# Hybrid encoder layer: a fixed order of operations and a fixed buffer for each tile in place of a list scheduler

## The chip, the cores and the metric

The kernel runs on one core of a Trainium2 chip. The metric is the time of one execution on the device in microseconds (us), the median over runs. The engines are TensorE (PE, with its weight loads as PEld), VectorE (DVE), ScalarE (ACT), GpSimd (POOL) and SyncE (SP), which issues most of the transfers. PSUM is the memory that PE writes, eight banks of 2 KB per partition; tiles lie in SBUF.

## The reference

One layer (SEQ 512, D_MODEL 1024, float32) of an encoder with two branches side by side, then a feed-forward part (FFN):

```python
h = rmsnorm(x, mix_norm)
p = h @ w_in
rx, ry, qkv, z, ba, gates = jnp.split(p, SPLIT_IDX, axis=-1)
y_rnn = rglru_branch(rx, ry, ...) @ w_rnn_proj     # conv, gates r and i, two linear scans (forward, backward)
y_dn = deltanet_branch(qkv, z, ba, ...) @ w_dn_proj
g_rnn, g_dn = jnp.split(jax.nn.sigmoid(gates), 2, axis=-1)
x = x + (g_rnn * y_rnn + g_dn * y_dn) @ w_out
h = rmsnorm(x, ffn_norm)
gt, up = jnp.split(h @ w_gate_up, 2, axis=-1)
x = x + (jax.nn.silu(gt) * up) @ w_down
return rmsnorm(x, final_norm)
...
# deltanet_branch, for each of 8 heads and 2 directions, over chunks of the sequence:
A = jnp.where(strict, jnp.einsum("nhcid,nhcjd->nhcij", kb, k) * decay, 0.0)
u = triangular_solve(A + eye, v * beta)            # unit lower triangle
w = triangular_solve(A + eye, kb * exp(gc))
S = S * exp(gl) + kd^T @ (u - w @ S)               # step from chunk to chunk
```

## The kernel before, in words

The whole layer is one function, `trunk`, with no loops left on the chip: about nine thousand operations in one long program. Each weight of 128 columns is loaded as 512 KB of float32 (`wraw`), ACT casts it to a rounded half (`hi`, in a `wx` or `t4` tile) and DVE makes the rest (`lo = raw - hi`). A product is then three matmuls, hi by hh, hi by hl and lo by hh, where `hh` and `hl` are the same two halves of the normalised and transposed input. The output projection and the two FFN products use forms with seven instead of eight partial products, whose sums of weight and input blocks are made on DVE; partial sums pass through DRAM tensors named `sums` and `osums`.

Where the program is in the chip's time:
- up to about 25 us, the head: four tiles of x are loaded, normalised, transposed on PE (`ax <- ident, t`) and split into hh and hl; `mm120` is the first input projection, `mm62` the narrow one of 32 columns for the DeltaNet's gates.
- to about 630 us, the input projections, and between them the recurrent branch and, head by head, the DeltaNet. Its triangular inverse (`dn_inverse`) stands at about 320, 420, 500 and 590 us: DVE solves 32-row blocks, then PE joins them in products of 32 by 32 and 64 by 64 (`ax <- t,na`, `ax <- t,t`), each step needing DVE or ACT to bring the result of the step before into SBUF. Other products with 512 columns stand between the steps as cover.
- to about 720 us, the output projections.
- from 720 to 940 us, gate and up (`in_w_gate_up`) with 256-column products, and with them the weights' sums; from 940 the down product, the last norm and the output.

No engine's order is that of the source. Each call on an engine goes through a recorder (`Rec`, line 384 for all of them, so that the profile groups by tiles and not by lines), which keeps the operation with a cost. `Plan.order` is a list scheduler: it plays the program through with those costs, with a lag from engine to engine, with the price of a table change on ACT, and with the transfers' time; whenever an engine is free, it picks among its ready operations the one with the earliest due time, if the tiles that it needs can be had. The due times come from a table by stage (`TIMES`), less 12 us (`AHEAD`) for the cast of a weight and 40 us for its load. The operations are then issued in that order, and the tile pools give each new tile a buffer of its kind and make it wait for the release of the buffer's last tile.

The kinds, with their numbers of buffers (`t2` holds 2 KB per partition, `t4`, `wraw` and `wx` 4 KB; `mm`, `ax` and `st` are banks of PSUM):

```python
N2, N4, NW = 15, 24, 4
...
raw = new(wp, shape, "wraw", NW)
hi = new(wp, shape, "wx", 4, F32R)
...
return new(ps, (P, 512), "mm", 3)
return new(ps, (P, 512), "ax", 3)
return new(ps, (P, 512), "st", 2)
```

A tile's name in the listings below is its kind, a running number and the number of the tensor (mm120_200); the same running number after the change is the same tile (ps120_197). In the profile the numbers are left out.

Of the kernel before, what the change touches and what calls it, by code (L numbers as in the profile page):

```python
# [7 lines left out]
F32 = mybir.dt.float32  # L8
# [22 lines left out]
SWITCH = 12000  # L31
WARM = 3400
RELEASE = 200
LOOK = 40
TIMES = [
# [14 lines left out]
]  # L50
ENGINES = ("PE", "DVE", "ACT", "POOL", "SP")
N2, N4, NW = 15, 24, 4
AHEAD = 12.0
# [6 lines left out]
class Plan:  # L60

    TABLES = {AF.Exp: ("exp",), AF.Tanh: ("exp", "sigmoid", "silu", "gelu"), AF.Sigmoid: ("sigmoid",), AF.Sqrt: ("sqrt",),
              AF.Ln: ("ln",), AF.Silu: ("silu",), AF.Gelu_apprx_tanh: ("gelu",)}

    LAG = {("PE", "PE"): 0, ("PE", "DVE"): 250, ("PE", "ACT"): 250, ("DVE", "PE"): 320, ("ACT", "PE"): 320, ("POOL", "PE"): 320,
           ("DVE", "DVE"): 130, ("DVE", "ACT"): 250, ("ACT", "ACT"): 50, ("ACT", "DVE"): 200, ("DVE", "POOL"): 250,
           ("POOL", "DVE"): 150, ("ACT", "POOL"): 250, ("SP", "SP"): 0}

    def __init__(self, nc):
        self.nc = nc
        self.ops = []
        self.where, self.bases = [], []
        self.t = self.base = 0.0
        self.stage = 0
        self.tags = {}
        self.tile_tag = {}
        self.hist = {}
        self.keep = set()  # L80
        self.extra = ()
        self.admit = ()

    def tile(self, pool, shape, dt, tag, bufs, name):
        ap = pool.tile(list(shape), dt, tag=tag, name=name, bufs=bufs)
        self.tile_tag[ap.tensor.name] = tag
        self.tags[tag] = bufs
        return ap

    @staticmethod  # L90
    def region(ap):
        t = ap.tensor
        name = t.name
        dims = list(ap.ap)
        if ap.space == PSUM:
            return name, 0, P, 1
        if ap.space == DRAM:
            lo = hi = ap.offset
            for s, n in dims:
                lo, hi = (lo, hi + s * (n - 1)) if s >= 0 else (lo + s * (n - 1), hi)  # L100
            return name, lo, hi + 1, 1
        pitch = 1
        for n in t.shape[1:]:
            pitch *= n
        p0, off = divmod(ap.offset, pitch)
        free = [(s, n) for s, n in dims[1:] if s != 0 and n > 1]
        free.sort(key=lambda d: abs(d[0]))
        starts, run = [off], 1
        for s, n in free:
            if s < 0:  # L110
                starts, s = [x + s * (n - 1) for x in starts], -s
            if s <= run:
                run = s * (n - 1) + run
            else:
                starts = [x + s * i for x in starts for i in range(n)]
        gran = max(1, pitch // 256)
        mask = 0
        for x in starts:
            a, b = x // gran, (x + run - 1) // gran
            mask |= ((1 << (b - a + 1)) - 1) << a  # L120
        return name, p0, p0 + dims[0][1], mask

    def add(self, eng, fn, outs, ins, cost, tail=0.0, table=None):
        i = len(self.ops)
        deps = set(self.extra)
        touched = {ap.tensor.name for ap in self.admit}
        for aps, write in ((ins, False), (outs, True)):
            for ap in aps:
                name, p0, p1, mask = self.region(ap)
                if name not in self.tile_tag and name not in self.keep:  # L130
                    continue
                touched.add(name)
                h = self.hist.setdefault(name, [])
                for j, q0, q1, m, w in h:
                    if (write or w) and j != i and q0 < p1 and p0 < q1 and m & mask:
                        deps.add(j)
        for aps, write in ((ins, False), (outs, True)):
            for ap in aps:
                name, p0, p1, mask = self.region(ap)
                if name not in self.tile_tag and name not in self.keep:  # L140
                    continue
                h = self.hist[name]
                if write:
                    h[:] = [r for r in h if not (p0 <= r[1] and r[2] <= p1 and r[3] | mask == mask) or r[0] == i]
                h.append((i, p0, p1, mask, write))
        self.ops.append((eng, fn, deps, touched, round(cost), round(1.25 * tail), table, self.t))
        self.where.append((self.stage, round(1e3 * (self.t - self.base))))
        self.bases.append(round(1e3 * self.base))

    def order(self):  # L150
        import heapq
        from bisect import insort
        ops = self.ops
        n = len(ops)
        when = []
        for (s, d), b in zip(self.where, self.bases):
            if s < len(TIMES):
                b, b0 = TIMES[s] * 100, b
            elif TIMES:
                b += max(TIMES) * 100 - b0  # L160
# [1578 lines left out]
```

## Time and profile before

| | us |
|---|---|
| median of 3 runs | 1052.1 (1052.09 to 1052.18) |
| span of the profiled execution, first to last instruction | 1051.0 |
| PE busy | 1037.1 (99%) |
| PEld busy | 905.0 (86%) |
| DVE busy | 869.5 (83%) |
| ACT busy | 706.7 (67%) |
| POOL busy | 75.7 (7%) |

Of the profiled execution the span is what the profile gives, and the durations below come from it. A matmul's end in the profile is modelled, so that its record is longer than the distance to the next one; the distance between starts is what a matmul costs in a dense stretch. Rows of groups give the operation, its output and inputs, its shape and number, the busy time and mean duration, and the idle time of the engine before it with its releaser. Rows of windows give the stretch and the busy time of PE, PEld, DVE, ACT and POOL (number of instructions in brackets), the granted clock, the share of the transfer engines and GB/s. Rows of the timeline and of the chain begin with the start and the duration.

### The profile page before, as it was taken

How to read it: one execution, taken by the hardware profiler on the slowest of the kernel's cores; microseconds unless marked ns; L12 is line 12 of the kernel's file. 1: busy time of each engine (PE TensorE's matmuls, PEld its weight loads, DVE VectorE, ACT ScalarE, POOL GpSimd, SP SyncE). 2: the span in 40 equal slices, each digit the busy share in tenths (PEclk: the TensorE clock that was granted, in tenths of full speed). 3: DMA queues.
4: the chain of work that ended last, by engine and by line, in shares of the span. 5: the costliest groups of instructions: out<-in, count | busy, mean ns of one | idle time of the engine just before them, and what ended most of it. 6: DMA issues, size and time to landing. Idle time of an engine off the chain costs nothing.

```text
span 1051.0 us, 17876 instructions
## 1 busy us (share of the span) xinstructions
PE 1037.1 (99%) x6707; PEld 905.0 (86%) x6707; DVE 869.5 (83%) x1626; ACT 706.7 (67%) x1287; POOL 75.7 (7%) x133
## 2 busy tenths in 40 slices
PE   8999999999999999999999999999999999999997
PEld 7888788888888987887888798889999999998886
DVE  7769989669794697489469657999999898989997
ACT  7799989787537877686875644668544454556574
POOL 2000000204100220211021000000000000000000
PEclk9999999999999999999999999999999999999999
DMA  9622222245233256559536564688453644336532
GB/s 278 196 79 81 61 75 75 71 112 148 81 100 91 73 144 150 158 133 218 122 76 145 169 172 140 197 256 292 129 171 102 200 139 130 109 110 207 197 123 80
DMA packets 180854, 146.95 MB, mean 140 GB/s; under 512 B 6784, under 2 KB 161552, under 8 KB 180768
## 3 DMA queue, kind: packets, MB, share of 16 engines
q1 hardware_dynamic: 175840, 129.95, 41.8%
q0 software_dynamic: 3744, 12.72, 6.5%
q10 hardware_dynamic: 1184, 3.15, 0.8%
q8 instruction: 52, 0.85, 0.3%
q14 instruction: 34, 0.28, 0.1%
HBM read 121.12 MB, written 12.09 MB: 127 GB/s over the span
## 4 chain that ended last, share of the span: by engine, by line
PE 86%; DVE 8%; ACT 2%; DMA 2%; issue 1%; SPq 1%; ACTq 0%; DVEq 0%
PE mm L384 49%; PE ax L384 23%; PE st L384 15%; DVE t L384 6%; ACT t L384 1%; DVE na L384 1%; DVE wx L384 1%; SPq L384 1%; DMA t<-in_w_down_dram 1%; DMA wraw<-in_w_in_dram 1%; DMA gain2r<-in_ffn_norm_dram 0%; ACT wx L384 0%; ACT ax L384 0%; ACTq L384 0%; ACT na L384 0%
## 5 line engine op out<-in xcount | busy, mean ns | idle before, releaser
L384 PE MATMUL mm<-hh,wx 128*128 128x512 f32 (+2 forms) x1280 | 368.8, 363 | 0.1
L384 DVE TENSOR_TENSOR t<-t,t 128x512 fp32r<-128x512 f32 (+25 forms) x501 | 249.3, 511 | 30.3 <-ACT t L384 20.7
L384 PEld LDWEIGHTS mm<-hh,wx 128*128 128x128 f32 (+1 forms) x1280 | 230.4, 188 | 35.4 <-ACT wx L384 0.7
L384 PE MATMUL mm<-hl,wx 128*128 128x512 f32 (+2 forms) x648 | 228.6, 362 | 0.0
L384 ACT CAST wx<-wraw 128x1024 fp32r<-128x1024 f32 (+3 forms) x139 | 129.9, 937 | 90.6 <-PE mm L384 32.9
L384 PE MATMUL ax<-t,t 128*128 128x512 f32 (+3 forms) x1134 | 156.9, 292 | 1.2 <-DVE t L384 1.2
L384 DVE TENSOR_TENSOR wx<-wraw,wx 128x1024 fp32r<-128x1024 f32 (+3 forms) x115 | 120.7, 1051 | 35.5 <-PE mm L384 16.8
L384 PEld LDWEIGHTS ax<-t,t 128*128 128x128 f32 (+1 forms) x1134 | 123.0, 161 | 21.6 <-issue 2.2
L384 PEld LDWEIGHTS mm<-hl,wx 128*128 128x128 f32 (+1 forms) x648 | 121.7, 188 | 16.8
L384 ACT CAST t<-t 128x512 fp32r<-128x512 f32 (+2 forms) x148 | 94.1, 653 | 44.5 <-DVE t L384 36.1
L384 PE MATMUL mm<-t,wx 128*128 128x512 f32 x480 | 116.6, 394 | 0.0
L384 PEld LDWEIGHTS mm<-t,wx 128*128 128x128 f32 x480 | 89.0, 188 | 18.4 <-issue 0.2
L384 DVE SCALAR_TENSOR_TENSOR t<-mm,par,t 128x511 f32<-128x511 f32 (+1 forms) x108 | 80.2, 744 | 20.9 <-ACT t L384 19.7
L384 ACT ACT_TABLE_LOAD x64 | 82.1, 1283 | 5.0 <-DVE t L384 2.3
L384 PE MATMUL mm<-t,t 128*128 128x256 f32 (+1 forms) x420 | 79.8, 330 | 0.1
L384 ACT ACTIVATE t<-t 128x128 f32<-128x128 f32 (+4 forms) x86 | 47.5, 559 | 41.0 <-DVE t L384 39.3
L384 PEld LDWEIGHTS mm<-t,t 128*128 128x128 f32 x420 | 63.8, 190 | 7.2 <-DVE t L384 0.5
L384 PE MATMUL st<-hh,wx 128*128 128x512 f32 (+1 forms) x224 | 67.7, 375 | 0.0
L384 ACT CAST t<-wraw 128x1024 fp32r<-128x1024 f32 (+1 forms) x55 | 49.2, 894 | 18.3 <-DMA wraw<-in_w_gate_up_dram 7.2
L384 DVE TENSOR_TENSOR t<-wraw,t 128x1024 fp32r<-128x1024 f32 (+1 forms) x55 | 56.3, 1023 | 5.3 <-ACT t L384 5.1
L384 PEld LDWEIGHTS st<-hh,wx 128*128 128x128 f32 x224 | 41.2, 188 | 7.6
L384 PE MATMUL st<-hl,wx 128*128 128x512 f32 (+1 forms) x112 | 41.5, 375 | 0.0
(195 smaller groups left out, 1519.1 us busy)
## 6 DMA issues: line engine op xcount, KB each, us to landing
wraw<-in_w_in_dram SPq DMA_DIRECT2D x72, 512.0 KB, 4.1
wraw<-in_w_gate_up_dram SPq DMA_DIRECT2D x44, 512.0 KB, 4.1
wx<-wraw POOLq DMA_DIRECT2D x24, 512.0 KB, 5.3
wraw<-in_w_out_dram SPq DMA_DIRECT2D x12, 512.0 KB, 4.5
wraw<-in_w_rnn_proj_dram SPq DMA_DIRECT2D x16, 384.0 KB, 3.5
t<-in_w_down_dram SPq DMA_DIRECT2D x11, 512.0 KB, 5.9
sums<-t SPq DMA_DIRECT2D x11, 512.0 KB, 5.0
wraw<-sums SPq DMA_DIRECT2D x11, 512.0 KB, 3.6
```

What stands on the lines that cost most here:

```text
L384: self.plan.add(e, lambda: real(*a, **kw), outs, ins, cost, tail, table)
```

## The change

The scheduler, its costs, its due times and all arguments that fed it (`after`, `admit`, `spend`, `ahead`) are taken out. In their place stand two tables. `ORDER` lists the numbers of the 9123 recorded operations in the order in which they are issued; by the change's own words it was searched with random transfer and vector delays. `HOMES` gives each tile of the kinds t2, t4 and PSUM one buffer by number: 16 homes of 2 KB, 32 of 4 KB, and 8 banks. The raw weights and their halves are now t4 tiles like the others (4 + 4 + 24 buffers before, 32 in one set after), and mm, ax and st are one set of eight banks (3 + 3 + 2 before). A home is a pool with one buffer; the program itself adds, for each engine that begins to use the buffer's new tile, a wait for the other engines' last use of the old one. The operations and their shapes are the same on every engine, apart from the waits and the table loads of ACT that the order entails: 74 of them instead of 64 in the listings. PE has 144 separate instructions for semaphore waits instead of 58.

```diff
-SWITCH = 12000
-WARM = 3400
-RELEASE = 200
-LOOK = 40
-TIMES = [
-    -162283, -159297, -163526, -108037, -92752, -158970, -94346, -59098, 168648, -70151, -72611, -51972, -22916,
...
-N2, N4, NW = 15, 24, 4
-AHEAD = 12.0
+ORDER = """
+2 15 16 17 18 19 0 126 5 3 7 122 20 21 22 23 24 10 12 11 8 283 1 25 26 27 28 13 14 29 30 9 129 31 32 33 34 111 127 113
...
+HOMES = """
...
-    def order(self):
...
+    def place(self, pool, shape, dt, home, name):
+        ap = pool.tile(shape, dt, tag=home, name=name, bufs=1)
+        self.home[ap.tensor.name] = home
+        return ap
+
+    def emit(self):
+        order = [int(i) for i in ORDER.split()]
...
+        info = mybir.DependencyInfo(mybir.DependencyClass.Sync, mybir.DependencyReason.ANTI)
+        now, users, before = {}, {}, {}
+        for i in order:
+            eng, names, run = self.ops[i]
+            ins = run().ins
+            for name in names:
+                home = self.home.get(name)
+                if home is None:
+                    continue
+                if now.get(home) != name:
+                    now[home] = name
+                    before[home], users[home] = users.get(home, {}), {}
+                if eng not in users[home]:
+                    for other, last in before[home].items():
+                        if other != eng:
+                            self.tc.add_manual_dep(ins, last.name, info, reason="the buffer's last use")
+                users[home][eng] = ins
...
     def new(pool, shape, tag, bufs, dt=F32):
-        return plan.tile(pool, shape, dt, tag, bufs, nm(tag))
+        if tag in ("t2", "t4", "ps"):
+            return plan.place(pool, list(shape), dt, f"{tag}h{next(homes)}", nm(tag))
+        return pool.tile(list(shape), dt, tag=tag, name=nm(tag), bufs=bufs)
...
-        return new(ps, (P, 512), "mm", 3)
+        return new(ps, (P, 512), "ps", 1)
...
     with tc.manual_schedule():
-        todo = plan.order()
-        for i in todo:
-            plan.ops[i][1]()
+        plan.emit()
```

Three places, as the listings of the two programs have them.

The first place is the head. On SP, before (t4117's raw weight is `wraw117`, that of the narrow projection `wraw60`; t411 to t414 are the tiles of x):

```order
1 L384 DMA t411_91<-in_x_dram 128x1024
2 L384 DMA t412_92<-in_x_dram 128x1024
3 L384 DMA wraw117_197<-in_w_in_dram 128x8x128
4 L384 DMA t413_93<-in_x_dram 128x1024
5 L384 DMA t414_94<-in_x_dram 128x1024
6 L384 DMA t2121_201<-in_rg_wa_dram 128x2x128
7 L384 DMA t2121_201<-in_rg_wx_dram 128x2x128
8 L384 DMA wraw60_140<-in_w_in_dram 128x8x32
9 L384 DMA wraw132_212<-in_w_in_dram 128x8x128
10 L384 DMA t2136_216<-in_rg_wa_dram 128x2x128
```

On SP, after:

```order
1 L508 DMA t411_88<-in_x_dram 128x1024
2 L508 DMA t412_89<-in_x_dram 128x1024
3 L508 DMA t4117_194<-in_w_in_dram 128x8x128
4 L508 DMA t460_137<-in_w_in_dram 128x8x32
5 L508 DMA t414_91<-in_x_dram 128x1024
6 L508 DMA t413_90<-in_x_dram 128x1024
7 L508 DMA t4132_209<-in_w_in_dram 128x8x128
8 L508 DMA t4102_179<-in_w_in_dram 128x8x128
9 L508 DMA t2136_213<-in_rg_wa_dram 128x2x128
```

The narrow weight moved from the eighth place to the fourth, ahead of the last two tiles of x, which changed places, and the recurrent gates' weights moved behind two more projections' weights. On PE in the head, before, from the last of the first twelve transposes on:

```order
14 L384 MATMUL ax35_115<-ident1_81,t428_108 128x128
15 L384 MATMUL mm120_200<-hh19_99,t4118_198 128x256
16 L384 MATMUL mm120_200<-hl20_100,t4118_198 128x256
17 L384 MATMUL mm120_200<-hh19_99,t4118_198 128x256
18 L384 MATMUL mm120_200<-hl20_100,t4118_198 128x256
19 L384 MATMUL ax36_116<-ident1_81,t421_101 128x128
20 L384 MATMUL ax36_116<-ident1_81,t428_108 128x128
```

On PE in the head, after, from the last transposes of the first two tiles on:

```order
17 L508 MATMUL ps35_112<-ident1_78,t421_98 128x128
18 L508 MATMUL ps35_112<-ident1_78,t428_105 128x128
19 L508 MATMUL ps120_197<-hh19_96,t4118_195 128x256
20 L508 MATMUL ps62_139<-hh19_96,t461_138 64x256
21 L508 MATMUL ps62_139<-hl20_97,t461_138 64x256
22 L508 MATMUL ps62_139<-hh19_96,t461_138 64x256
23 L508 MATMUL ps120_197<-hl20_97,t4118_195 128x256
24 L508 MATMUL ps120_197<-hh19_96,t4118_195 128x256
```

All sixteen transposes of the first two tiles now stand ahead of the first projection, and the narrow projection's products (ps62) stand between its products instead of behind them.

The second place is the first step of the triangular inverse in the first of its four places, on PE; before (bank 495 holds the first product of the step, bank 497 the second, which needs it in SBUF as t2496):

```order
1113 L384 MATMUL ax495_575<-t2492_572,na479_559 32x32
1114 L384 MATMUL ax495_575<-t2493_573,na479_559 32x32
1115 L384 MATMUL mm445_525<-t4414_494,wx447_527 128x512 x2
1116 L384 MATMUL mm445_525<-t4420_500,wx447_527 128x512 x2
1117 L384 MATMUL ax497_577<-t2493_573,t2496_576 32x32
1118 L384 MATMUL ax497_577<-t2492_572,t2496_576 32x32
```

And after:

```order
1181 L508 MATMUL ps495_572<-t2493_570,na479_556 32x32
1182 L508 MATMUL ps473_550<-t4408_485,t4476_553 128x512
1183 L508 MATMUL ps473_550<-t4414_491,t4476_553 128x512
1184 L508 MATMUL ps473_550<-t4420_497,t4476_553 128x512
1185 L508 MATMUL ps473_550<-t4432_509,t4476_553 128x512
1186 L508 MATMUL ps473_550<-t4438_515,t4476_553 128x512
1187 L508 MATMUL ps473_550<-t4444_521,t4476_553 128x512
1188 L508 MATMUL ps560_637<-hh19_96,t4559_636 128x512 x4
1189 L508 MATMUL ps498_575<-t2496_573,t2493_570 32x32
```

Four products of 512 columns stood between the two steps, and ten do now; the two banks that the second step fills (497 and 498) are now filled together.

The third place is in the FFN, on PE, where one bank (1684) gets two products one after the other and DVE empties it in between. Before, from the end of the first one to the begin of the second:

```order
3685 L384 MATMUL ax1684_1764<-t41217_1297,t41678_1758 128x256 x4
3686 L384 MATMUL ax1683_1763<-hh1082_1162,t41677_1757 128x256
...
3694 L384 MATMUL ax1683_1763<-hh1082_1162,t41678_1758 128x256 x4
3695 L384 MATMUL mm1659_1739<-hh1082_1162,wx1651_1731 128x256
3696 L384 MATMUL mm1659_1739<-hl1083_1163,wx1651_1731 128x256
3697 L384 MATMUL ax1684_1764<-t41223_1303,t21679_1759 128x256
```

After, the end of the first product in bank 1684, and the begin of the second:

```order
4024 L508 MATMUL ps1684_1761<-t41217_1294,t41678_1755 128x256 x2
4025 L508 MATMUL ps1683_1760<-t41219_1296,t41675_1752 128x256
...
4098 L508 MATMUL ps1660_1737<-t41221_1298,t41654_1731 128x256 x2
4099 L508 MATMUL ps1681_1758<-hh1082_1159,t41674_1751 128x256
4100 L508 MATMUL ps1684_1761<-t41223_1300,t21679_1756 128x256
```

Fourteen products of 256 columns stood between the two uses of the bank, and now some 76 rows do.

More of the change, by code (lines that the diff above doesn't have):

```diff
@@ L28 @@
 EPS = 1e-6
-SWITCH = 12000
-WARM = 3400
-RELEASE = 200
-LOOK = 40
-TIMES = [
[14 rows of a table removed]
-]
-ENGINES = ("PE", "DVE", "ACT", "POOL", "SP")
-N2, N4, NW = 15, 24, 4
-AHEAD = 12.0
+ORDER = """
[387 rows of a table added]
+"""
+HOMES = """
[37 rows of a table added]
+"""
 LASTK = 3
@@ L60 @@
 class Plan:
[L64 to L87, printed above, removed]
-        return ap
@@ L90, in region @@
[L90 to L130, printed above, removed]
-                    continue
[L132 to L148, printed above, removed]
@@ L318, in elems, with __init__ @@
-def elems(ap):
-    n = 1
-    for s, m in list(ap.ap)[1:]:
-        n *= m
-    return n
+    def __init__(self, tc):
+        self.tc, self.ops, self.home = tc, [], {}
+    def place(self, pool, shape, dt, home, name):
+        ap = pool.tile(shape, dt, tag=home, name=name, bufs=1)
+        self.home[ap.tensor.name] = home
+        return ap
+    def emit(self):
+        order = [int(i) for i in ORDER.split()]
+        if sorted(order) != list(range(len(self.ops))):
+            raise RuntimeError("the order is not one of these operations")
+        info = mybir.DependencyInfo(mybir.DependencyClass.Sync, mybir.DependencyReason.ANTI)
[6 more added lines that the diff above has]
+                if home is None:
+                    continue
+                if now.get(home) != name:
[6 more added lines that the diff above has]
+                users[home][eng] = ins
@@ L334, in call @@
         def call(*a, **kw):
-            args = list(a) + list(kw.values())
-            aps = [x for x in args if hasattr(x, "ap") and hasattr(x, "tensor")]
-            out = kw.get("out", a[0] if a else None)
-            outs = [out] + ([kw["accum_out"]] if kw.get("accum_out") is not None else [])
-            ins = [x for x in aps if not any(x is o for o in outs)]
-            big = [x for x in ins if elems(x) > 1 or x.space == PSUM]
-            n = max([elems(out)] + [elems(x) for x in ins])
@@ L384, in call @@
-            self.plan.add(e, lambda: real(*a, **kw), outs, ins, cost, tail, table)
+            names = {x.tensor.name for x in list(a) + list(kw.values()) if hasattr(x, "ap") and hasattr(x, "tensor")}
+            self.plan.ops.append((self.eng, names, lambda: real(*a, **kw)))
         return call
@@ L1202, in out_sums @@
     def out_sums(j):
-        spend(0.1)
-        now = plan.t
-        ra, rb, s_ = new(wp, (P, 2, 512), "wraw", NW), new(wp, (P, 2, 512), "wraw", NW), four()
-        plan.t = now - 40
+        ra, rb, s_ = new(t4, (P, 2, 512), "t4", 1), new(t4, (P, 2, 512), "t4", 1), four()
         Q.dma_start(ra, wo[:, j, 0, :].rearrange("p (h n) -> p h n", h=2))
         Q.dma_start(rb, wo[:, j, 1, :].rearrange("p (h n) -> p h n", h=2))
-        plan.t = now
         V.tensor_tensor(s_[:, 0, :], ra[:, 0, :], ra[:, 1, :], ALU.add)
@@ L1228, in trunk @@
             dn_z(g)
-        spend()
         dn_out(g)
@@ L1310, in halves @@
     def halves(src, own=False):
-        hi, lo = (new(wp, (P, 2, 512), "wx", 4, F32R) if own else four(F32R) for _ in range(2))
-        parts_of(src, hi, lo, 0)
+        hi, lo = (new(t4, (P, 2, 512), "t4", 1, F32R) if own else four(F32R) for _ in range(2))
+        parts_of(src, hi, lo)
         return [(hi[:, i, :], lo[:, i, :]) for i in range(2)]
     def out_w(j):
-        now = plan.t
-        ra, rs = new(wp, (P, 2, 512), "wraw", NW), new(wp, (P, 2, 512), "wraw", NW)
-        plan.t = now - 40
+        ra, rs = new(t4, (P, 2, 512), "t4", 1), new(t4, (P, 2, 512), "t4", 1)
         Q.dma_start(ra[:, 0, :], wo[:, j, 0, 0:512])
@@ L1465, in gate_up @@
     def gate_up(n):
-        spend(10.2)
-        now = plan.t
-        rg, ru = new(wp, (P, 8, P), "wraw", NW), new(wp, (P, 8, P), "wraw", NW)
-        plan.t = now - 40
+        rg, ru = new(t4, (P, 8, P), "t4", 1), new(t4, (P, 8, P), "t4", 1)
         Q.dma_start(rg, wg[:, :, n * P:(n + 1) * P])
```

440 lines of the change are left out of this document (69 added, 371 removed), and 436 rows, old and new, of tables (HOMES, ORDER, TIMES).

## The prediction

> **What bounds the kernel now.** I read the page first, then the windows of 25 us, the chain that ended last, the groups by shape, and last the timeline at the places where the windows show the PE short. The head of the page:
>
> ```profile
> span 1051.0 us, 17876 instructions
> PE 1037.1 (99%) x6707; PEld 905.0 (86%) x6707; DVE 869.5 (83%) x1626; ACT 706.7 (67%) x1287; POOL 75.7 (7%) x133
> PEclk9999999999999999999999999999999999999999
> PE 86%; DVE 8%; ACT 2%; DMA 2%; issue 1%; SPq 1%; ACTq 0%; DVEq 0%
> ```
>
> The span is 1051.0 us and the median of the runs 1052.1, so 1.1 us lie outside the span; I keep them. PE is busy nearly all the time at the full clock in every slice. The change leaves every PE instruction as it is, so the first question is how much of the 1051.0 an order can touch at all. For that the busy share is no use, because a matmul's end is modelled; I use the distance between matmuls in dense stretches, from the chain:
>
> ```profile
> 277.53 45.33 PE mm L384 x200
> 748.64 2.88 PE mm L384 x24
> ```
>
> The first is 200 products of 512 columns: 45.33/200 = 0.227 us each. The second is 24 products of 256 columns: 0.120 us each. The groups by shape give the counts (first and last of the nine 512-column groups, then the largest of 256 and the small ones):
>
> ```profile
> L384 PE MATMUL mm<-hh,wx 128*128 128x512 f32 x912 | 293.6, 395 | 0.1
> L384 PE MATMUL st<-wx,t 128*128 128x512 f32 x90 | 23.2, 389 | 0.0
> L384 PE MATMUL mm<-hh,wx 128*128 128x256 f32 x352 | 70.8, 283 | 0.0
> L384 PE MATMUL ax<-ident,t 128*128 128x128 f32 x178 | 27.3, 275 | 0.7 <-DVE t L384 0.5 <-ACT ax L384 0.2
> L384 PE MATMUL ax<-t,t 32*32 32x32 f32 x384 | 4.9, 196 | 0.0
> ```
>
> All groups of a kind together: 2901 products of 512 columns make 657.7 us, 2066 of 256 columns 247.9, 64 slow ones of 256 columns about 14, and 758 of 128 columns with the 896 small tiles about 97 (0.11 each by their starts, 0.01 to 0.03 for the small ones). The sum is 1016 us of work that no order removes. The first useful transpose and the last products of the program:
>
> ```profile
> 7.51 0.69 PE L384 MATMUL ax<-ident,t 128*128 128x128 f32 x3
> 1043.13 1.24 PE L384 MATMUL st<-t,t 128*128 128x256 f32 x9
> ```
>
> The ninth of the last row starts 8 times 0.12 after the first, at 1044.1. From 7.51 it is some 1037 us, so about 21 us are lost between matmuls. Of these some 5.5 go where tiles of 32 and 64 rows change with full ones, which any order pays. About 15 us are waits, and with the ends of the span (7.5 before, 6.9 after) they are all there is to win. The windows say where a part of them is, PE being the first engine and its busy time in the second column behind the stretch:
>
> ```profile
> 7.30:25.00 17.70, 15.64 (x113) 13.59 (x113) 14.70 (x33) 15.70 (x34) 0.54 (x1) 1.00 1.10 291
> 100.00:125.00 25.00, 24.99 (x108) 19.67 (x107) 24.69 (x31) 24.91 (x35) 0.00 (x0) 1.00 0.35 96
> 475.00:500.00 25.00, 24.32 (x172) 19.93 (x171) 21.95 (x64) 16.66 (x26) 3.44 (x5) 1.00 0.96 213
> 775.00:800.00 25.00, 25.00 (x211) 25.00 (x210) 25.00 (x46) 12.39 (x23) 0.00 (x0) 1.00 0.46 137
> 875.00:900.00 25.00, 23.82 (x198) 23.62 (x198) 21.36 (x41) 10.03 (x20) 0.00 (x0) 1.00 0.45 136
> ```
>
> PE lacks 2.06 us in the head, 0.68 before 500 and 1.18 before 900. A wait of less than about 0.16 us does not show at all, since a record lasts 0.39 us and the next product follows after 0.227; such small ones are the difference between these rows and the 15.
>
> A rule weighed against this: the Trainium skill, page "Perfetto Trace Analysis", section "Identifying the Most-Contended Engine", calls matmul busy time a bad measure and takes the weight loads' busy share (and the share of peak) instead. By it 14% of the span, some 146 us, would be open. The trace agrees on the first half (99% busy holds 21 us of loss) and not on the second: in the row 100 to 125, where products of 512 columns stand back to back, the weight loads fill only 19.67 of 25, so 86% is near full here.
>
> **The change part by part.** *The operations.* The same operations with the same shapes are issued on every engine, so the 1016 us stay: cost 0, bounds 0 and 0. Only the order, and which buffer a tile gets, differ.
>
> *The head.* What PE and SP do there before:
>
> ```profile
> 8.66 1.20 PE L384 MATMUL ax<-ident,t 128*128 128x128 f32 x9 [0.45 <-DVE t L384]
> 9.77 0.38 PE L384 MATMUL mm<-hh,t 128*128 128x256 f32 x1
> 10.96 0.39 PE L384 MATMUL mm<-hl,t 128*128 128x256 f32 x1 [0.81 <-DVE hl L384]
> 13.93 0.38 PE L384 MATMUL mm<-hl,t 128*128 128x256 f32 x1 [0.50 <-DVE hl L384]
> 7.24 4.52 SPq L384 DMA_DIRECT2D t<-in_rg_wa_dram  x1
> 0.80 0.86 SPq L384 DMA_DIRECT2D t<-in_x_dram  x2
> ```
>
> PE runs twelve transposes, then goes into the first projection (mm120), whose products alternate between hh and hl and so wait each time DVE has made the next hl. The narrow projection (mm62, the gates' 32 columns), which needs only the same hh and hl, comes behind it. The new order runs all sixteen transposes first and interleaves the narrow products with the first projection, so a wait for hl finds others to run. The three idle pieces of 0.45, 0.81 and 0.50 make 1.76 of the 2.06. I take −2.0. At best the small waits and some of the last hl's lateness go too: −4.9. On the other side, the 128 KB of the narrow weight are now ahead of the last two x tiles on SP's queue; an issue there takes 0.43 us (the row of two x tiles), and everything behind it in the queue is that much later: +0.4 at worst. The transfer at 7.24, which holds SP's queue for 4.52 us, is the tenth there before and the ninth now, so what is queued behind it moves little: 0.
>
> *The steps of the inverse.* In four places (about 320, 420, 500 and 590 us) a chain of small products goes PE, DVE, PE. The cover between them is 512-column products. One place shows a wait:
>
> ```profile
> 498.54 0.74 PE L384 MATMUL ax<-t,na 32*32 32x32 f32 x64 [0.68 <-DVE t L384]
> 499.21 1.20 PE L384 MATMUL mm<-hh,wx 128*128 128x512 f32 x4
> 500.56 0.64 PE L384 MATMUL ax<-t,t 32*32 32x32 f32 x51
> ```
>
> The first row is the wait ahead of a chain's first product. Behind that product's step, five covering ones go from 499.21 to 500.56, 1.35 us where their spacing makes 1.13: 0.2 us lost that no idle time shows, and some of it is the change of tile size. In the first of the four places 4 covering products stand there before (0.9 us) and 10 after (2.3); between later steps 9 became 11, and 6 became 12. Eight chains of three such steps at 0.2 would be 4.8 us in all. Over the whole program the listings show the same: places where less than 0.5 us of PE work stands between the last matmul that a reader waits for and the next one that needs the reader fall from 216 to 156, and under 1 us from 464 to 302, about a third. Of the 15 us of waits some 4 are in the head (seen and unseen) and 2 in the rows of the FFN, leaving about 9 in between; a third of these would be −3, all of them −9, and none 0. A new tight place would cost what the row at 498.54 costs: five of those +3.4. I take −3.5, a little over the third, as the inverse's steps, where the 4.8 lies, gain more than the average.
>
> Small tiles now border on full tiles or on each other 53 times instead of 43, and fifteen times 32-row tiles stand beside 64-row ones, which the trace doesn't show. By the 0.2 us lost at 500.56 a border costs at most that. Ten more make +2.0, and as many saved by the direct neighbours −2.0: I take 0.
>
> *The FFN.* The 1.18 us before 900 come from this:
>
> ```profile
> 897.64 1.70 PE L384 MATMUL ax<-t,t 128*128 128x256 f32 x12 [1.18 <-DVE t L384]
> 897.17 0.42 DVE L384 TENSOR_TENSOR t<-ax,t 128x256 f32<-128x256 f32 x1
> 894.83 1.22 DVE L384 TENSOR_TENSOR wx<-wraw,wx 128x1024 fp32r<-128x1024 f32 x1
> 892.67 0.62 ACT L384 CAST t<-wraw 128x512 fp32r<-128x512 f32 x1 [3.63 <-DMA wraw<-in_w_gate_up_dram]
> ```
>
> Bank 1684 holds one product, DVE adds it into SBUF, and PE wants to fill the bank with the next one. The DVE add stood behind a weight subtraction of 1.22 us and two more, which were late because their raw load was late. Two things change: 14 products (1.7 us) stood between the two uses of the bank, and now some 76 rows (9 us) do; and the raw loads may sit in any of 32 buffers of 4 KB, not in four of their own. So −1.2, and at worst 0 if DVE is late elsewhere. Against it, eight other banks in the FFN are refilled 0.96 to 1.20 us after their last product, where before none was under 1.44. The reader takes 0.37 to 0.42, so alone it fits. It misses when its engine is inside a cast:
>
> ```profile
> 886.18 0.37 ACT L384 COPY t<-mm 128x256 f32<-128x256 f32 x1 [1.87 <-PE mm L384]
> 893.20 1.04 ACT L384 CAST wx<-wraw 128x1024 fp32r<-128x1024 f32 x1
> ```
>
> A 1.04 us cast just begun makes a refill late by about 0.3 to 0.8. ACT is under half busy there (10.03 of 25), so I price one or two of the eight: +0.5, with bounds 0 and 8 times 1.18 = +9.4. The term is −0.7.
>
> *Table loads.* The listing of ACT has 74 of them and not 64.
>
> ```profile
> L384 ACT ACT_TABLE_LOAD x64 | 82.1, 1283 | 5.0 <-DVE t L384 2.3
> ```
>
> Ten more are 12.8 us of ACT, which is idle a third of the time; they hide behind PE except from 50 to 125 us, where ACT is at 24.91 of 25 and gets two more. What hides them there is that PE has whole projections to run ahead; if that cover is gone, two loads are +2.6. I take 0, bounds 0 and +2.6. The Trainium skill, page "ScalarE: Activation LUTs", section "What ACT_TABLE_LOAD costs", adds a drain of about 1380 ns to the load's 1283, 2.66 us for each switch, which speaks against the change: ten would be 26.6 us by it. The trace agrees with the 1283; idle time just before the loads is only 5.0 us for 64, so a drain of that size does not show as idle time there.
>
> *More waits to issue.* PE gets 144 separate semaphore waits and not 58. Behind one stand the next matmuls, and who waits for these is DVE and ACT. In the trace, spacing around such a wait that is already met stays 0.227 or 0.120, so 0; bounds 0 and 86 times 0.02 = +1.7, an estimate from the pieces called issue in the chain of waits, which are 0.02 to 0.04 long.
>
> *The tail.* On DVE one write of 256 columns now stands ahead of the last bank's addition:
>
> ```profile
> 1044.54 0.42 DVE L384 TENSOR_TENSOR na<-st,na 128x256 f32<-128x256 f32 x1
> 1045.42 0.88 DVE L384 SCALAR_TENSOR_TENSOR na<-na,rin,t 128x256 f32<-128x256 f32 x2
> ```
>
> Half of that 0.88 piece, 0.44, moves ahead. DVE has the same work up to the end, but the square and the root that follow the addition begin up to 0.44 later: +0.2, bounds 0 and +0.4.
>
> **Sum.** −2.0 −3.5 −0.7 +0.2 = −6.0: span 1045.0, time 1046.1 us.
>
> **The rivals.** *The waits all go.* For it: the new order has longer covers everywhere I looked. Against: a transfer or a late reader only moves a wait. All 15 us gone make 1051.0 − 15 + 0.2 + 1.1 = 1037.3; down to 1040 I count as this case.
>
> *The order doesn't do what it says.* The PE is 99% busy, what is late at one place is late at another, and the gains of the head are eaten by the tail and new tight places: 1050 to 1054. For it: only 3.9 us of PE idleness are in plain rows. Against: the head's 1.76 us depend on what stands next on PE, and that has changed.
>
> *The tight banks of the FFN.* With a fixed bank for each product, PE stops at a refill until ACT or DVE has emptied it, and everything behind on PE stops too, though other work is ready. At 1.18 for each place, seven of the eight missed outweigh the 6.5 us won elsewhere and it ends slower; if all miss and waits like the row at 498.54 come at ten more places, it is 1052.1 − 6.5 + 9.4 + 6.8 = 1061.8, and with the eight alone 1055.0. For it: the row at 897.64 is just such a wait, with more room (1.7 us) than these have. Against: DVE and ACT find gaps in 900 to 925, where PE lost nothing.
>
> ```profile
> 900.00:925.00 25.00, 25.00 (x211) 25.00 (x210) 20.86 (x37) 11.30 (x20) 0.00 (x0) 1.00 0.36 106
> ```
>
> **How the numbers follow.** A measurement of this kernel can tell from no change what is over about 0.2%, that is 2.1 us. The forecast, 1040 to 1050, gets 0.50, since its two largest terms have rows and listings behind them. All waits gone (under 1040) gets 0.13, no effect 0.15, the tight banks 0.22, as the price of one miss is seen and their number isn't. So faster 0.63, same 0.15, slower 0.22. The likeliest gives 1046; its own range is 1040 to 1050. The range for 8 in 10 leaves out about a tenth at each end: 1038.5, near the floor, and 1056, just beyond the eight missed banks.
>
> **What would show it.** Right: the window 7.30 to 25 with PE over 17 of 17.7; no wait at the first small products of the inverse; no PE wait for DVE between 875 and 900; the span between 1039 and 1049. Wrong: PE waits of about 1 us with an ACT copy or a DVE add as releaser spread over 740 to 940 (the banks); PE waits behind table loads between 50 and 125; or the head's first projection starting later than 9.77, if x now lands later. If the windows of the middle show the same losses at other places, the third taken from counting was wrong.

## The result, and the profile after

The changed kernel takes 1054.7 us (median of 11 runs, 1052.9 to 1056.3) against 1052.2 before (11 runs, 1050.5 to 1052.7): a ratio of 1.0026, with a 95% interval of 1.0017 to 1.0034. It is slower by about 2.6 us. The prediction was 1046, so the time did not fall by 6 us, it rose.

The head of the page of the kernel after, to be read beside that of before:

```profile
span 1052.7 us, 17920 instructions
PE 1039.9 (99%) x6707; PEld 910.1 (86%) x6707; DVE 879.9 (84%) x1626; ACT 716.2 (68%) x1297; POOL 74.7 (7%) x133
PE 91%; ACT 7%; issue 1%; POOL 0%; DMA 0%; DVE 0%; DVEq 0%; SPq 0%; POOLq 0%; ACTq 0%
```

The chain that ended last is the line to look at. Before, 8% of it went through DVE and 2% through ACT; now 7% goes through ACT and nothing through DVE. Something on ACT stands in PE's way.

To find the place I worked out one number from the starts of all matmuls in each trace: how late a matmul starts, which is its start less the time that all matmuls ahead of it take in a dense stretch (0.227 us for 512 columns, 0.120 for 256, 0.11 for 128, 0.05 and 0.02 for the small tiles). Where it grows, PE lost time.

| up to | before | after | after less before, added in the stretch |
|---|---|---|---|
| 25 us | 9.52 | 8.90 | −0.62 |
| 225 us | 11.86 | 10.93 | −0.31 |
| 275 us | 13.50 | 16.82 | +4.25 |
| 625 us | 16.75 | 21.78 | +1.71 |
| last matmul | 19.22 | 21.57 | −2.68 |
| end of span behind the last matmul's start | 6.94 | 6.22 | −0.72 |

The sum is +1.63, the difference of the two spans (1052.66 and 1051.03). The execution of before that was profiled was a long one: in the runs that show spans, before has 1048.7 to 1051.5, mostly about 1050, so the usual difference is nearer 2.7.

So the head, the FFN and the tail did gain. Of the loss, 4.25 of 5.96 us lie in one stretch of 50 us, and the rest between 275 and 625, where the small tiles are. The windows of after, at the places quoted before and at the place of the loss:

```profile
7.30:25.00 17.70, 16.89 (x117) 15.83 (x116) 13.35 (x29) 12.71 (x29) 1.05 (x3) 1.00 1.10 297
225.00:250.00 25.00, 24.86 (x109) 20.01 (x107) 21.55 (x19) 21.12 (x27) 7.91 (x7) 1.00 0.49 132
252.00:256.00 4.00, 3.46 (x9) 2.77 (x10) 2.02 (x2) 3.98 (x9) 1.14 (x2) 0.61 0.76 218
875.00:900.00 25.00, 25.00 (x211) 25.00 (x210) 23.31 (x44) 9.42 (x18) 0.00 (x0) 1.00 0.54 156
```

The column behind POOL's is the granted clock: 0.61 between 252 and 256. (The first row's 1.00 is not the whole truth; the section on the prediction comes back to it.) The timeline of PE there:

```profile
252.54 0.50 PE L508 MATMUL ps<-hh,t 128*128 128x512 f32 x1 [2.68 <-ACT t L508]
254.12 0.63 PE L508 MATMUL ps<-hh,t 128*128 128x512 f32 x1
254.54 0.63 PE L508 MATMUL ps<-hl,t 128*128 128x512 f32 x1
```

PE waited 2.68 us for ACT, and then products of 512 columns follow each other by 0.42 us and not by 0.227. The timeline of ACT and POOL shows what it waited for:

```profile
244.11 0.99 ACT L508 ACTIVATE t<-t,ngc 128x128 f32<-128x128 f32 x3
244.93 3.10 POOL L508 TENSOR_SCALAR_AFFINE_SELECT t<-t 128x512 f32<-128x512 f32 x1 [8.84 <-ACT t L508]
248.47 2.65 POOL L508 TENSOR_SCALAR_AFFINE_SELECT t<-t 128x512 f32<-128x512 f32 x2
251.15 0.40 ACT L508 ACTIVATE t<-t,ngc 128x128 f32<-128x128 f32 x1 [4.81 <-POOL t L508]
251.46 1.03 ACT L508 CAST t<-t 128x1024 fp32r<-128x1024 f32 x1
```

Read from the bottom: PE's product needs the cast of its weight, which ends at 252.49. The cast stands in ACT's queue behind an exponential, which waits 4.81 us for a select on POOL. That select stands on POOL behind another one that had waited 8.84 us for an exponential on ACT. And that exponential was late, as the groups of ACT between 225 and 250 say, first before, then after:

```profile
L384 ACT ACT_TABLE_LOAD x2 | 2.6, 1283 | 0.0
```

```profile
L508 ACT ACT_TABLE_LOAD x7 | 9.0, 1283 | 0.1
```

Seven table loads where there were two, because the order alternates between square roots, gelus and exponentials.

### The profile page after: what moved, and what is told of

Same layout as the page of the kernel before. It is cut to its first block, busy times and chain, and to the rows that moved or that the text cites. A ratio compares the mean times of both kernels' runs of the same rounds, so it can differ in the third digit from the quotient of the medians.

```text
span 1052.7 us, 17920 instructions
## 1 busy us (share of the span) xinstructions
PE 1039.9 (99%) x6707; PEld 910.1 (86%) x6707; DVE 879.9 (84%) x1626; ACT 716.2 (68%) x1297; POOL 74.7 (7%) x133
## 4 chain that ended last, share of the span: by engine, by line
PE 91%; ACT 7%; issue 1%; POOL 0%; DMA 0%; DVE 0%; DVEq 0%; SPq 0%; POOLq 0%; ACTq 0%
PE ps L508 91%; ACT t L508 3%; ACT L508 2%; ACT ps L508 1%; ACT na L508 0%; POOL t L508 0%; DMA t<-in_x_dram 0%; ACT hh L508 0%; DVE hl L508 0%; DVE t L508 0%; DVE na L508 0%; DVEq L1749 0%; SPq L508 0%; DVE rin L508 0%; ACT drt L508 0%
## 5 line engine op out<-in xcount | busy, mean ns | idle before, releaser
L508 DVE TENSOR_TENSOR t<-t,t 128x512 fp32r<-128x512 f32 (+14 forms) x779 | 487.3, 654 | 48.2 <-ACT t L508 35.0
L508 PE MATMUL ps<-hh,t 128*128 128x512 f32 (+2 forms) x1824 | 500.8, 351 | 2.9 <-ACT t L508 2.9
L508 PE MATMUL ps<-t,t 128*128 128x512 f32 (+3 forms) x2895 | 495.7, 317 | 0.3 <-ACT t L508 0.3
L508 PEld LDWEIGHTS ps<-t,t 128*128 128x128 f32 (+1 forms) x2895 | 404.8, 179 | 52.9 <-ACT t L508 2.1
L508 ACT CAST t<-t 128x512 fp32r<-128x512 f32 (+2 forms) x382 | 285.5, 786 | 121.9 <-DVE t L508 68.3
L508 PEld LDWEIGHTS ps<-hh,t 128*128 128x128 f32 (+1 forms) x1824 | 326.1, 190 | 46.4 <-ACT t L508 4.0
L508 PE MATMUL ps<-hl,t 128*128 128x512 f32 (+2 forms) x920 | 306.8, 351 | 0.1
L508 PEld LDWEIGHTS ps<-hl,t 128*128 128x128 f32 (+1 forms) x920 | 173.3, 190 | 21.8 <-DVE hl L508 0.6
L508 DVE SCALAR_TENSOR_TENSOR t<-ps,par,t 128x511 f32<-128x511 f32 (+2 forms) x116 | 84.8, 744 | 30.7 <-ACT t L508 28.4
L508 ACT ACTIVATE t<-t 128x128 f32<-128x128 f32 (+5 forms) x110 | 72.7, 668 | 35.1 <-DVE t L508 29.0
```

Of the source, the lines that this page charges most:

```text
L508: self.plan.ops.append((self.eng, names, lambda: real(*a, **kw)))
```

## The experiments

Ratios are to the kernel before on the same chip (its median there was 1051.4 to 1051.9).

**The old order on fixed buffers.** ORDER is replaced by the order that the scheduler of before gave, HOMES by buffers chosen for it.

```diff
-2 15 16 17 18 19 0 126 5 3 7 122 20 21 22 23 24 10 12 ...
+12 0 10 2 5461 111 1 3 4 8 5 11 6 7 112 9 122 123 124 ...
```

> The order of before, issued by the machinery of after: each tile has a fixed buffer (16 of 2 KB, 32 of 4 KB and 8 banks in one set each), chosen as the one that had been free longest in the trace of before. It parts the two halves of the change. Theory (the order lost the time, the buffers cost nothing): within 1 us of before, 1051.2 to 1053.2, and no PE wait of over 2 us between 225 and 275. Rival (the fixed homes and their added waits cost the time): 1054 to 1055, as after.

Measured: 1049.25 us, ratio 0.9976 (0.9966 to 0.9986). Neither was right: the old order on fixed buffers is faster than before by 2.5 us. So the two halves of the change have opposite signs: buffers about −2.5, order about +5.2 (1.0026 less 0.9976, of 1052), each order on a table of buffers of its own. Its windows:

```profile
475.00:500.00 25.00, 24.67 (x259) 20.05 (x260) 21.72 (x63) 16.28 (x27) 3.26 (x4) 1.00 0.93 221
875.00:900.00 25.00, 25.00 (x211) 25.00 (x210) 24.10 (x45) 11.73 (x22) 0.00 (x0) 1.00 0.44 128
```

The wait of 1.18 us near 896 is gone with the buffers alone; the place did not need the new order.

**Another table of buffers for the new order.** HOMES is replaced, ORDER kept.

```diff
-0 1 9 8 1 0 4 3 0 7 6 3 2 5 4 26 ... 12 7 15 5 2 11 1 6 11 2 6 2 13 ...
+0 1 9 8 1 0 4 3 0 7 6 3 2 5 4 26 ... 12 7 15 5 2 6 2 11 6 1 1 2 3 ...
```

1491 of the 1778 numbers differ.

> The order of after with another choice of buffers: for each tile the buffer of its kind that had been free longest in the trace of after (1491 of 1778 tiles get another one). Theory (after loses by its order, not by its buffers): the wait of 2.7 us near 252 and the slow clock behind it are still there, 1053.5 to 1055. Rival (the table of buffers sets the wait): 1051 or less.

Measured: 1053.7 us, ratio 1.0016 (1.0007 to 1.0025). The wait is there, 2.63 us at 252.84 (the timeline of PE), and the slow clock behind it (0.63 in the window):

```profile
252.84 0.67 PE L508 MATMUL ps<-hh,t 128*128 128x512 f32 x1 [2.63 <-ACT t L508]
```

```profile
252.00:256.00 4.00, 3.15 (x8) 2.48 (x9) 2.21 (x2) 3.98 (x9) 0.48 (x1) 0.63 0.80 209
```

The wait and the clock stay with the order, whichever of the two tables it runs on.

**The cast moved ahead.** One number of ORDER, the cast of the weight, moves one place.

```diff
-... 2136 2037 2044 2046 2610 ...
+... 2136 2037 2044 2610 2046 ...
```

> After, with one number of the order moved: ACT's cast of a weight (251.46 in the trace of after) is issued ahead of the exponential in front of it, which waits 4.81 us for POOL. Theory (PE's wait of 2.68 us at 252.5 is that cast's place in ACT's queue, and the slow clock behind it follows from the wait): the cast ends at about 247.4, the wait goes, the granted clock stays at 1.00 from 252 to 256, and the time falls by 2.7 + 1.8 = 4.5, to about 1050.2. Rival (ACT as a whole is too late there, so that the next cast is what PE waits for): under 1 us won, a wait of over 1 us a few us later.

Measured: 1052.1 us, ratio 1.0005 (0.9996 to 1.0014), 0.002 or 2.2 us better than after: half of what was expected. The wait for the cast and the slow clock are gone, but PE waits a little later for the exponentials behind the select, 0.46 and 0.94 us (its timeline of PE, then of ACT):

```profile
252.71 1.56 PE L508 MATMUL ps<-t 128*128 128x256 f32 x6 [0.46 <-ACT t L508]
255.22 1.13 PE L508 MATMUL ps<-t 128*128 128x256 f32 x4 [0.94 <-ACT t L508]
250.61 1.57 ACT L508 ACTIVATE t<-t,ngc 128x128 f32<-128x128 f32 x5 [3.92 <-POOL t L508]
```

Both theories had a part: the place in the queue was the larger wait, and ACT behind POOL was late all the same.

**The table loads grouped.** Four numbers of ORDER move, so that operations of one table stand together.

```diff
-... 1721 1733 2017 1739 ... 2013 1727 1299 ... 1828 3415 ... 2018 2022 2014 2016 ...
+... 1721 1733 1727 2017 1739 ... 2013 1299 ... 2018 2022 2014 1828 3415 ... 2016 ...
```

> After, with ACT's operations between 225 and 245 moved so that those of one table stand together: a square root ahead by four places, and a select and two exponentials ahead of a gelu. Four fewer table loads stand ahead of the exponential that POOL's select at 244.93 waits for; the cast stays behind the exponential that waits for POOL. Theory (the table loads made POOL late and so the cast): POOL's selects move ahead by 4 to 5 us, PE's wait goes and with it the slow clock, 1050 to 1051. Rival (only the place in the queue matters, the loads are hidden): ACT still waits 3 to 5 us for POOL and PE for the cast, 1054 to 1055.

Measured: 1051.3 us, ratio 0.9994 (0.9985 to 1.0003), 3.4 us better than after, though the cast still stands behind the exponential. POOL's selects come when their data do:

```profile
237.50 1.26 POOL L508 TENSOR_SCALAR_AFFINE_SELECT t<-t 128x512 f32<-128x512 f32 x1 [1.57 <-ACT t L508]
240.22 2.68 POOL L508 TENSOR_SCALAR_AFFINE_SELECT t<-t 128x512 f32<-128x512 f32 x2 [1.10 <-DMA t<-gcr]
```

The select that ran at 244.93 with 3.10 us now starts at 237.50 and takes 1.26. The exponentials that stood at 244.11 on ACT come 8.0 us earlier:

```profile
236.09 1.28 ACT L508 ACTIVATE t<-t,ngc 128x128 f32<-128x128 f32 x4
```

Three table loads stand ahead of them in that stretch instead of seven, which is 5.1 of the 8.0 us at 1.28 each; most of the rest is a gelu and a cast that now stand behind them. In the whole program only two loads are gone (72 instead of 74). So ACT's lateness was the first cause, and the queues of POOL and ACT passed it on to PE. The table loads are the larger part of that lateness; the place of the exponentials in the queue is the smaller, and the two were not tried apart. Nor was it tried why the select took 1.84 us longer before. By the measure of the first table, the stretch from 225 to 275 loses 3.6 us less than in after. A new wait of 0.87 us stood at 232 (1.03 by the starts of the matmuls, as the expectations below have it).

**The wait filled.** Twelve extra matmuls of 512 columns stand in the place of the wait; this is additional work, overwritten by the product behind it.

```diff
+            for run in [self.fill] * (12 if i == 2612 else 0) + [run]:
...
+        plan.fill = lambda: nc.tensor.matmul(plan.bank, hh[:, 0, 0:P], hh[:, 0, :], start=True, stop=True)
```

> After, with twelve more matmuls of 512 columns in front of the product that waits at 252.54, into the bank which that product then overwrites; they read only hh. They take 12 times 0.227 = 2.7 us, which is the wait. Theory (the wait itself brings the clock down to 0.61 for 4 us): the cast comes no earlier, but the clock stays at 1.00 and some 1.8 us are won: about 1052.9. Rival (the clock falls there for another reason, or by the load of all engines): no gain, 1054.7, and the clock under 0.7 between 252 and 256.

Measured: 1055.3 us, ratio 1.0041 (1.0028 to 1.0054), five runs, one of them 1059.0. The clock stayed at 1.00, as the window says; the timeline of PE has the twelve matmuls and a later wait:

```profile
252.00:256.00 4.00, 4.00 (x20) 3.33 (x19) 1.99 (x2) 3.98 (x9) 1.16 (x2) 1.00 0.79 222
```

```profile
250.10 2.88 PE L1728 MATMUL ps<-hh 128*128 128x512 f32 x12
506.95 0.50 PE L511 MATMUL ps<-hh,t 128*128 128x512 f32 x1 [2.04 <-issue]
```

At 300 us the matmuls are 4.15 us less late than in after; 12 times 0.227 = 2.72 of that is the extra work, which counts as work here, and 1.4 is the clock. So the clock's part is shown, and the time is not: 2.04 us are lost at 506, behind a burst of small tiles, in a wait with no releaser in the profile. After has 0.2 us of that kind at the same place. What PE waits for there stays open, and it was not tried. A candidate is that PE waited for its own instructions: a queue marked "instruction" (q8) brings 16 KB about every 120 matmuls, and ahead of this wait it did so at 475.8 and then, 253 matmuls later, at 504.3, 0.6 us before PE went idle. In after 214 matmuls lie between the two, and in the small_grouped run, which has no such wait, 165.

**The small products grouped**, on top of the grouped table loads. In the inverse, 64-row products that stood between 32-row ones move behind these.

```diff
-... 2236 2186 2188 2189 2190 2192 2237 2194 2195 ... 2218 2219 2220 2242 2243 ...
+... 2186 2188 2189 2190 2192 2194 2195 ... 2218 2219 2220 2236 2237 ... 2242 2243 ...
```

> The kernel with grouped table loads (1051.25), and on PE the 64-row products of the inverse that stood between 32-row ones moved behind the last of these: 17 of 64 products, in three of the four places. A border between 32 and 64 rows takes 0.12 to 0.15 us in the trace of after, where two equal neighbours take 0.01 to 0.05, and 15 of them go. Theory (the borders cost what they show): 15 times about 0.1 = 1.5 us less, about 1049.8. Rival (they hide a wait for DVE that then shows): no gain within 0.5 us.

Measured: 1049.0 us, ratio 0.9975 (0.9965 to 0.9986); 0.0019, or 2.0 us, from the step before. The timeline of after shows what went: between 327.18 and 329.29 the two kinds take turns, and each turn costs more than its products.

```profile
327.18 0.33 PE L508 MATMUL ps<-t,na 64*64 64x64 f32 x2
327.44 0.31 PE L508 MATMUL ps<-t,t 32*32 32x32 f32 x10
327.68 0.33 PE L508 MATMUL ps<-t,na 64*64 64x64 f32 x2
327.93 0.31 PE L508 MATMUL ps<-t,t 32*32 32x32 f32 x10
```

Five 32-row products (ten records) take 0.24 us from 327.44 to 327.68, and one 64-row product 0.26. In the starts of all records, from 32 to 64 rows it is 0.12 us, back 0.15, and between two equal ones mostly under 0.05. The trace of the grouped kernel has 3 such borders where after has 15: 12 at about 0.12 is 1.4 us, somewhat less than the 2.0 measured. The trace of the step before also has a wait of 0.66 us without a releaser at 504.79, and the grouped kernel's has none there.

**The buffers kept apart by kind**, all on the old order; only HOMES differs (its first numbers, from the first experiment to each). First all kinds apart, then the banks alone, then the 4 KB buffers alone.

```diff
-0 1 3 4 0 1 9 6 2 11 10 2 3 4 6 19 15 10 21 16 ...     (nothing apart)
+8 9 10 11 3 4 13 12 2 15 14 5 3 4 5 21 18 10 22 19 ... (all apart)
+0 1 3 4 3 4 9 6 2 11 10 5 3 4 5 19 15 10 21 16 ...     (banks)
+8 9 10 11 0 1 13 12 2 15 14 2 3 4 6 21 18 10 22 19 ... (4 KB)
```

> The order of before on fixed buffers, as in the run with the old order, but the buffers kept apart by kind as before: 3, 3 and 2 banks, 4 raw, 4 halves and 24 others of 4 KB, 15 of 2 KB. A control. If sharing the buffers is what won 2.5 us there: as before, 1051 to 1052.5, with the wait of over 1 us near 896 back. If the way of waiting (a wait for the last use only, instead of a pool's release) won it: 1049 to 1049.8, as with the old order and shared buffers.

> The same with only the banks kept apart (3, 3 and 2) and the 32 buffers of 4 KB shared. Theory (the loads gain, since four raw buffers made SP wait, and the banks do nothing): 1049 to 1050, no wait near 896. Rival (eight shared banks give PE room): 1051 to 1052.

> The same with only the 4 KB buffers kept apart (4 raw, 4 halves, 24 others) and the eight banks shared. Theory (the loads gain): 1051 to 1052, with the wait near 896 back. Rival (the banks gain): 1049 to 1050.

| kinds kept apart | ratio | 95% interval | PE wait near 895 |
|---|---|---|---|
| banks and 4 KB | 0.9986 | 0.9977 to 0.9994 | none |
| banks | 0.9979 | 0.9970 to 0.9988 | none |
| 4 KB | 0.9990 | 0.9981 to 0.9999 | 1.05 us |
| none (first experiment) | 0.9976 | 0.9966 to 0.9986 | none |

The wait came back in one of the two that should have it (the timeline of PE with the 4 KB buffers apart):

```profile
895.67 1.58 PE L506 MATMUL ps<-t,t 128*128 128x256 f32 x11 [1.05 <-DVE t L506]
```

Sharing the eight banks does nothing that can be seen (first and third row, second and fourth). Sharing the 32 buffers of 4 KB is worth about 0.001, which is about the width of the intervals. The control, which shares nothing, still wins 0.0014: some of the gain lies in which buffer of a kind is taken (here the one free longest in the trace), or in waiting for a last use in place of a pool's release. These two were not tried apart, so which of them it is stays open.

**Three attempts at a better kernel that missed.** The first moves the cast ahead of the gelu on top of both groupings, for the wait of 0.87 us at 232; the second moves the gelu instead; the third gives the old order the last 265 operations in the new order.

```diff
-... 1721 1733 1727 ... 1797 1740 ...
+... 1721 1733 1727 ... 1740 1797 ...     (first)
+... 1797 1721 1733 1727 ... 1740 ...     (second)
```

> The kernel with grouped table loads and grouped small products, and ACT's cast of a weight at 233 moved ahead of the gelu and its table load, 1.9 us earlier. There PE waited 1.03 us at 232.3. Theory (what is left of the loss near 230 is again a cast behind a table load): that wait goes, a ratio of 0.9965, 1.0 us better than with the two groupings alone. Rival (PE then waits at the next cast or bank): 0.9975.

> The kernel with both groupings, and the gelu at 232.9 (it empties a bank that PE wants) moved ahead of the three square roots, with its table load; the cast stays behind. When the cast was moved instead, PE's wait at 231 grew to 2.9 us and ended with the gelu, so the gelu, not the cast, is taken to be what it waits for. Theory: the wait of 1.03 us goes, a ratio to before of 0.9965. Rival (what needs the square roots, now 1.9 us later, makes PE wait): 0.9975 or above.

> The old order on shared fixed buffers (1049.25) up to the operations that start by 1010 us there, and the 265 operations behind them in the order of after. From the last matmul's start to the end of the span it is 7.2 us with the old order and 6.2 with the new one. Theory (the new tail, which puts one 256-column write ahead of the last bank's addition and the rest behind the square, is worth 1 us by itself): a ratio to before of about 0.9966, 0.001 under that of the old order on shared buffers. Rival (the shorter tail belongs to what the new order has left undone by 1040): the ratio stays at 0.9976.

Measured: 1.0017 (1.0008 to 1.0026), 0.9986 (0.9977 to 0.9994) and 0.9985 (0.9976 to 0.9994). In the first, the cast now stood ahead of the gelu and waited for its own load, and PE waited 2.90 us for ACT, up to the end of the gelu at 234.69, which empties a bank (its timeline); the clock fell again, to 0.57 (its window):

```profile
231.73 1.04 ACT L508 CAST t<-t 128x1024 fp32r<-128x1024 f32 x1 [0.98 <-DMA t<-in_w_in_dram]
234.74 0.80 PE L508 MATMUL ps<-hh,t 128*128 128x512 f32 x1 [2.90 <-ACT t L508]
```

```profile
234.00:238.00 4.00, 3.26 (x8) 2.61 (x9) 3.96 (x4) 3.96 (x9) 1.50 (x2) 0.57 0.00 0
```

In the second, that wait went and another of 0.85 us for DVE came at 245.94. In the third, a wait of 0.85 us for DVE stands at the seam (1008.87); behind the last matmul's start 6.7 us are left, between the old order's 7.2 and the new one's 6.2. Each is the same lesson: a wait was moved, not removed.

The two best kernels are the old order on shared fixed buffers (0.9976) and the new order with table loads and small products grouped (0.9975). They cannot be told apart.

## Why the prediction was wrong, step by step

Two steps failed: the table loads, which the sum had at nothing, and the waits in the middle, which were to give most of the gain.

- **Table loads, taken as 0 with bounds 0 and +2.6: the step that turned the sign.** The reason given, that ACT is idle a third of the time and PE has projections to run ahead, is an average. The cover was looked at only between 50 and 125 us; five of the added loads lie between 225 and 250, where POOL and PE wait for ACT in turn. Cost: +4.25 us in 225 to 275, of which 2.68 is the wait and 1.4 to 1.7 the clock; moving four operations took 3.6 of it away. The 26.6 us for ten loads by the rule of the Trainium skill (page "ScalarE: Activation LUTs", section "What ACT_TABLE_LOAD costs") were too many, but its direction, against the change, was right.
- **The inverse and the middle, −3.5 with bounds −9 and +3.4: wrong.** Measured −0.3 between 25 and 225 and +1.7 between 275 and 625. "About 15 us are waits" failed first. By the table above before does lose 7.2 us between 25 and 625, near the 9 that the prediction put there, but the waits proper among them are about 0.8 at 498 and 0.4 at 536, by the starts (1.3 more are at 896); the rest lies in many pieces under 0.3 us, the borders of small tiles among them. Counting places with little cover counted what was not lost in waits. The new order also has a wait of its own, 0.54 us for ACT at 433.11.
- **Small tiles, 0 with bounds −2.0 and +2.0:** near the upper bound. Ten more borders were counted, and as many savings were set against them without a row. Grouping took 2.0 us away, 1.4 of it by the spacing of the borders.
- **The head, −2.0:** measured −0.6 by the lateness at 25 us. The waits for hl went, and one of 0.68 us among the transposes came. What the prediction left out is PE's clock there, which the distances show and the clock column does not:

```profile
3.09 4.63 PE L384 MATMUL ax<-ones 128*128 128x128 f32 x20
1.05 4.63 PE L508 MATMUL ps<-ones 128*128 128x128 f32 x20 [1.05 <-POOL eps_t L508]
7.01 0.90 PE L508 MATMUL ps<-ident,t 128*128 128x128 f32 x3 [1.12 <-DVE t L508]
13.09 0.41 PE L508 MATMUL ps<-hl,t 128*128 128x256 f32 x1
13.30 0.41 PE L508 MATMUL ps<-hh,t 128*128 128x256 f32 x1
8.66:12.07 3.41, 3.41 (x16) 3.09 (x17) 2.18 (x4) 3.26 (x8) 1.05 (x3) 0.50 1.01 301
```

  The first row is before, the next four are after, the last is a window of the kernel with grouped table loads. Twenty products of a tile of ones, whose result nobody needs, ran up to the first transposes before. In the new order they begin 2 us earlier, and PE waits 1.12 and 0.68 us for DVE behind them. The transposes from 8.59 on then stand 0.213 us apart, and the 256-column products up to 13.9 too, where before has 0.109 from 8.7 on and about 0.12. The trace of after has no record of the clock ahead of 13.96, so its 1.00 says nothing there; where there is one, as in the last row, the same distances go with 0.50. All eight traces of the new order have this, up to 11.5 to 14.6 us, and in the six of the old order it ends by 8.5. So the rise of PE's busy time in the window from 7.30, by 1.25 us, is in part products that took longer. At twice the distance these matmuls take about 2 us more, an estimate of the most that the clock cost there, since PE might have waited for DVE instead; no run puts the ones back. The first projection began at 11.27 and not 9.77, one of the prediction's signs of being wrong.
- **The FFN, −0.7:** better than said. From 725 to 925 before lost 1.89 us and after 0.03. The eight tight banks, the rival that was to make it slower, never made PE wait; but the gain is the buffers', as the old order shows. (The price of a miss, "about 0.3 to 0.8", comes out of its own rows as 0.2 to 0.5; it played no part.)
- **The tail, +0.2:** −0.7. The write put ahead of the last addition filled time in which DVE had nothing else: its reciprocal starts 1.25 us behind the end of the last addition before, and 0.84 after. The other 0.3 us were not followed up.
- **More waits to issue, 0:** no sign of a cost in dense stretches.
- **The 1.1 us outside the span** set one execution's span, 1051.0, against a median of others. In runs that show both, 1.7 to 1.8 us lie outside for before and mostly 1.9 to 2.0 for after. So the sum began with a span some 0.7 us too high and added some 0.7 us too little for the outside, and the two errors cancelled.

The chance of slower, 0.22, was on the wrong mechanism: not a bank, but a chain ACT, POOL, ACT, PE. That 1054.7 lies below the 1056 at the upper end of the range is luck, for that end was worked out from eight missed banks, and none was missed.

## What to carry to other kernels

When an order changes, count ACT's table loads by stretch and not in total, and follow who waits behind them: a load on an engine with idle time is free only where nobody is queued behind it. Before calling the difference between span and dense work "waits", take out the spacing between unlike tiles, which no order hides. And test the halves of a change apart: here a gain of 2.5 us from the buffers was hidden by a loss of 5.2 from the order.

## What the runs showed of the hardware

In three traces a PE wait of 2.6 to 2.9 us was followed by a lower granted clock: after waits of 2.68, 2.63 and 2.90 us it was 0.61, 0.63 and 0.57 over the next 4 us, and 512-column products followed each other by 0.42 to 0.43 us. In after it was 0.50 for 3.41 us:

```profile
252.89:256.30 3.41, 3.41 (x10) 2.67 (x9) 1.40 (x2) 3.38 (x8) 1.23 (x2) 0.50 0.76 218
```

After single waits of 0.85 to 1.18 us in dense stretches it stayed at 1.00, and so it did behind the 2.04 us at 506 in the filled kernel and when the 2.7 us were filled with matmuls. In the head two waits close together were enough: in the kernel with grouped loads 1.28 and 1.01 us, ending at 6.97 and 8.53, are followed by 0.50 from 8.66 to 12.07. The Trainium skill, page "TensorE: Matmul & The Clock Gate", section "What's actually happening", tells of half the clock after an idle window of about 3.4 us; the halving agrees (0.42 against 0.227 us), but a shorter wait than that brought it here. So a wait of that length costs some 1.4 to 1.7 us more than itself: 1.4 is what filling it won, and 1.7 is half of 3.41.
